# A decoder block's first stage: scale columns queued in a row, x turned by quarters, first weights asked for by GpSimd

## The chip, the cores and the metric

The kernel runs on one core of a Trainium2 chip. The metric is the device time of one execution in microseconds (us); less is better. The core has TensorE (PE, matmuls), VectorE (DVE), ScalarE (ACT), GpSimd (POOL) and SyncE (SP, which here only issues transfers); each works off its own queue in order and waits on semaphores for the others. 16 DMA engines move data between the chip's memory and the core's.

## The reference, cut to what matters

One layer for 512 tokens of width 2048, all in float32: an adaLN modulation, a normalised input, one input projection for two head groups, their mix, an output projection and an MLP. The change lies in the first lines of it.

```python
mod = silu(c) @ w_ada + b_ada            # 6 x 2048: shift, scale, gate for both halves
h = rms_norm(x, norm1_w) * (1 + scale) + shift
z = h @ w_in                             # 2048 -> 7168: q, k, v | q, f, i, g of the second group
...                                      # dilated attention | HGRN2, merged, w_out, gated residual
...                                      # second adaLN, squared-ReLU MLP, gated residual
```

The code names the column of (1 + scale) * norm1_w `g1c` and that of the shift `s1c`, 16 columns of 128 values each.

## The kernel before

**Exact products.** A float32 product is made of three reduced ones: every operand is split into a rounded part (`hi`, `whi`; ScalarE, L336 and L39) and what is left (`lo`, `wlo`; VectorE, L337 and L40), and TensorE adds hi x whi, lo x whi and hi x wlo (`ch_mm`, L206 to L208). Weights come in pairs of 128-row blocks (`load_w`, L189, 512 or 256 columns); the tiles for the rounded and for the remaining part number four each, and a pair of both groups' weights fills them.

**The first stage.** `gemv` makes modulation columns: for a block of columns it loads `w_ada` (L123) and adds 16 row blocks, each times a column of silu(c), on VectorE into two accumulators (the first two rows by L127, the rest by L129). A scale block is 256 columns, 8 loads of 256 KB and 16 VectorE operations; there are eight, and each serves two of the 16 row blocks k of x. `to_cols` turns the accumulators on TensorE (L149), sums them on ScalarE (L152), and `mod_cols` adds the bias and multiplies by the norm's weight on VectorE (L167, L169). x comes in 16 tiles; its squares are summed (L261, L264, L265), the inverse root is a power on GpSimd (L212), the tiles are scaled (L277 on ScalarE, L279 on VectorE), turned (64 transposes, L283) and copied (L285). `scaled(k)` multiplies a turned tile by its column (L335) and splits it.

**The first groups.** `first_groups` runs twice over k = 0..15 in pairs. The first pass takes 512 columns of the forget gate (`prj`) and 256 of the query (`prc`) of the second group, without the shift: 36 matmuls of 128x512 a pair, 288 in all. `before` (`scale_block`) makes the next scale block ahead of each pair. The second pass takes the next columns; during both, the shift columns are made in the background (`bg_step`, `shift_gen`: 512 columns at a time). What the first pass lacked, the shift's part, is made by `shift_through`: a gemv over `w_in`, whose accumulators are added (L143) and turned (L149). Then comes the rest of the input projection with its TensorE order written out by hand, the attention, the recurrence, the output projection and the MLP.

**What sets the order.** A scheduler places the instructions of the first stage in the order of the code, moved by the due times it works out; `tc.issue_after(ins)` holds what is made inside it behind an instruction. Buffers come from pools of fixed sizes, so a load or a split waits for the last reader of the tile that it overwrites. All weight and modulation loads of this stage are issued by SyncE, from one queue.

Of the kernel before, what the change touches and what calls it, by code (L numbers as in the profile page):

```python
# [15 lines left out]
P = 128  # L16
D = 2048
# [27 lines left out]
def hybrid_block(ctx, tc, x, c, positions, norm1_w, w_ada, b_ada, w_in, q_norm_w, k_norm_w,  # L45
# [29 lines left out]
    pool.memset(mhalf, -0.5)  # L75
# [10 lines left out]
    dve.tensor_copy(bcol, ps_c[:, 2 * NK:P])  # L86
    sc = const.tile([P, NK], F32, name="sc")
# [28 lines left out]
    def gemv(view, vec, col0, n=512, early=False):  # L116
# [3 lines left out]
        for k0 in range(0, NK, nk):  # L120
            raw = spare.pop(0) if early and spare else slot("araw") if early else gv.tile([P, 512], F32, name="araw", bufs=4)
            raw = raw.rearrange("p (k n) -> p k n", n=n)
            nc.sync.dma_start(raw, view[:, k0:k0 + nk, col0:col0 + n])  # L123
            for k in range(k0, k0 + nk):
                acc = accs[k % 2]
                if k < 2:
                    dve.tensor_scalar(acc, raw[:, k - k0], vec[:, k:k + 1], None, op0=ALU.mult)  # L127
                else:
                    dve.scalar_tensor_tensor(acc, raw[:, k - k0], vec[:, k:k + 1], acc, op0=ALU.mult, op1=ALU.add)  # L129
# [8 lines left out]
    def to_cols(accs, dst):  # L138

        nb = accs[0].shape[1] // P  # L140
        parts = 1 if nb == 4 else 2
        if parts == 1:
            dve.tensor_tensor(accs[0], accs[0], accs[1], op=ALU.add)  # L143
        yield
        pc = bank("pc")
        for j in range(nb):
            for u in range(parts):
                c = (j * parts + u) * P
                pe.transpose(pc[:, c:c + P], accs[u][:, j * P:(j + 1) * P], ident)  # L149
        for j in range(nb):  # L150
            c = pc[:, j * parts * P:(j + 1) * parts * P]
            act.activation(c, c, AF.Copy, accum_out=dst[:, j:j + 1])  # L152
# [7 lines left out]
    def mod_cols(kind, b, dst, nw, n=512, early=False):  # L160

        for _ in gemv(ada_v, sc, kind * D + b * n, n, early):
            yield
        nb = n // P
# [3 lines left out]
        if nw is not None:  # L168
            mod_cols.last = dve.scalar_tensor_tensor(d, d, 1.0, nw[:, b * nb:(b + 1) * nb], op0=ALU.add, op1=ALU.mult)  # L169
# [16 lines left out]
    def load_w(view, k0, c0, n=512, eng=None, ahead=True, raws=None):  # L186
        with tc.high_priority() if ahead else ExitStack():
            raw = wr.tile([P, 2, n], F32, name="wraw", tag="raw", bufs=4)
            nc.sync.dma_start(raw, view[:, k0:k0 + 2, c0:c0 + n])  # L189
# [20 lines left out]
    def rstd_of(dst, ss, n, inv_n):  # L210
        dve.tensor_scalar(dst, ss, inv_n, EPS, op0=ALU.mult, op1=ALU.add)
        pool.tensor_tensor(dst, dst, mhalf[:, 0:n], op=ALU.pow)  # L212
# [34 lines left out]
    first_scale = mod_cols(1, 0, g1c, n1c, 256, True)  # L247
# [8 lines left out]
    for q in range(4):  # L256
        for ti in range(NT):
            jk = work("jk")
            with tc.issue_after(sc_ready.ins), tc.issue_after(sig_ready.ins):
                if q == 3 and ti % 2:  # L260
                    dve.tensor_tensor_reduce(jk, xs[ti][q], xs[ti][q], op0=ALU.mult, op1=ALU.add, scale=1.0, scalar=0.0,  # L261
                                             accum_out=ssx[:, ti, q:q + 1])
                else:
                    act.activation(jk, xs[ti][q], AF.Square, accum_out=ssx[:, ti, q:q + 1])  # L264
    dve.tensor_reduce(rx, ssx, axis=AX.X, op=ALU.add)  # L265
# [1154 lines left out]
```

## Time and profile before

| | us |
|---|---|
| median of 3 runs | 2300.57 |
| lowest, highest | 2293.37, 2303.32 |
| the profiled execution | 2297.95 |
| its span | 2296.2 |
| TensorE busy | 2224.9 (97%) |
| VectorE busy | 1809.9 (79%) |
| ScalarE busy | 1098.2 (48%) |
| GpSimd busy | 447.3 (19%) |

An engine's queue is in order: an instruction that waits holds up all behind it. The table of groups gives for each kind of instruction its count, its mean duration and the idle time ahead of it with what ended that. In the timeline a row gives start, length, engine, line, operation, what it writes and reads, a count, and in brackets the idle time before it with its releaser. In the windows PEclk is the share of full clock that was granted to TensorE. Consecutive matmuls overlap, so their spacing is taken from starts.

### The profile page before, as it was taken

What the parts mean: (1) busy time and instruction counts of PE and PEld (TensorE: products, weight loads), DVE (VectorE), ACT (ScalarE), POOL (GpSimd) and SP (SyncE); (2) the same over time, 40 slices, a digit from 0 to 9 for tenths busy, and PEclk for the clock granted to TensorE, in tenths of its full rate; (3) what the DMA queues carried; (4) which work ended last, traced back from release to release, by engine and by line L of the source; (5) the groups of instructions that cost most, each with busy time, mean ns of one, the idle gap of its engine ahead of it and who ended that gap; (6) DMA issues with size and microseconds to landing.
All of it is one profiled execution on the core that took longest, in us unless ns stands there. A gap on an engine that the chain in (4) does not pass through costs nothing.

```text
span 2296.2 us, 33105 instructions
## 1 busy us (share of the span) xinstructions
PE 2224.9 (97%) x11769; PEld 1824.4 (79%) x11769; DVE 1809.9 (79%) x2765; ACT 1098.2 (48%) x1950; POOL 447.3 (19%) x664
## 2 busy tenths in 40 slices
PE   4899999999999999999999999999999999999999
PEld 3787877888778888778887888888888888888887
DVE  6999777677876565668648988988897679967878
ACT  5555434433344454447544556555564333343332
POOL 1000022000230000002232323323332222222221
PEclk9999999999999999999999999999999999999999
DMA  9798455556545256746969799889889987998784
GB/s 327 254 335 315 124 177 156 177 160 207 187 151 184 68 173 225 247 152 217 367 231 383 251 344 347 298 306 386 298 328 390 339 293 260 385 344 291 278 301 164
DMA packets 262582, 598.31 MB, mean 261 GB/s; under 512 B 23220, under 2 KB 43968, under 8 KB 262416
## 3 DMA queue, kind: packets, MB, share of 16 engines
q1 hardware_dynamic: 186800, 332.54, 43.1%
q0 software_dynamic: 70720, 254.21, 30.0%
q10 hardware_dynamic: 4896, 9.44, 1.2%
q8 instruction: 93, 1.52, 0.3%
q14 instruction: 73, 0.60, 0.1%
HBM read 518.49 MB, written 77.61 MB: 260 GB/s over the span
## 4 chain that ended last, share of the span: by engine, by line
PE 60%; DVE 17%; DMA 14%; issue 6%; ACT 2%; POOL 1%; SPq 0%; DVEq 0%; ACTq 0%; POOLq 0%
PE f L1177 9%; PE f L1178 9%; PE f L1176 9%; DMA araw<-in_w_ada_dram 6%; PE prj L198 5%; PE prj L199 5%; PE prj L200 5%; DVE vlo L1161 3%; DVE acc L129 3%; DVE raw L1144 2%; PE f L208 2%; PE f L206 2%; PE f L207 2%; DMA Fl<-f_lod 2%; DVE wlo L40 2%
## 5 line engine op out<-in xcount | busy, mean ns | idle before, releaser
L1160 ACT CAST vhi<-raw 128x1024 fp32r<-128x1024 f32 x392 | 413.4, 1055 | 534.5 <-PE f L1178 416.3
L1161 DVE TENSOR_TENSOR vlo<-raw,vhi 128x1024 fp32r<-128x1024 f32 x392 | 475.5, 1219 | 153.5 <-ACT vhi L1160 152.7
L1177 PE MATMUL f<-vlo,Fh 128*128 128x512 f32 x1376 | 537.1, 390 | 3.9 <-DVE vlo L1161 3.8
L1178 PE MATMUL f<-vhi,Fl 128*128 128x512 f32 x1376 | 535.8, 389 | 0.8 <-DMA Fl<-f_lod 0.8
L1176 PE MATMUL f<-vhi,Fh 128*128 128x512 f32 x1376 | 536.1, 390 | 0.0
L39 ACT CAST whi<-wraw 128x512 fp32r<-128x512 f32 (+1 forms) x368 | 219.8, 601 | 453.2 <-PE prj L200 313.3
L198 PE MATMUL prj<-whi,hi 128*128 128x512 f32 x896 | 364.9, 407 | 1.3 <-ACT gg L701 1.3
L200 PE MATMUL prj<-whi,lo 128*128 128x512 f32 x896 | 351.4, 392 | 0.0
L199 PE MATMUL prj<-wlo,hi 128*128 128x512 f32 x896 | 351.0, 392 | 0.0
L40 DVE TENSOR_TENSOR wlo<-wraw,whi 128x512 fp32r<-128x512 f32 (+1 forms) x368 | 243.2, 665 | 120.9 <-ACT whi L39 118.3
L129 DVE SCALAR_TENSOR_TENSOR acc<-araw,sc,acc 128x512 f32<-128x512 f32 (+1 forms) x392 | 252.7, 672 | 100.5 <-DMA araw<-in_w_ada_dram 99.2
L1177 PEld LDWEIGHTS f<-vlo,Fh 128*128 128x128 f32 x1376 | 258.3, 188 | 63.3 <-DVE vlo L1161 10.0
L1178 PEld LDWEIGHTS f<-vhi,Fl 128*128 128x128 f32 x1376 | 258.3, 188 | 54.8 <-DMA Fl<-f_lod 1.6
L1176 PEld LDWEIGHTS f<-vhi,Fh 128*128 128x128 f32 x1376 | 258.3, 188 | 53.5
L1144 DVE TENSOR_TENSOR raw<-raw,raw 128x1024 f32<-128x1024 f32 x224 | 267.7, 1216 | 4.1 <-DMA raw<-in_w_ff_dram 3.9
L198 PEld LDWEIGHTS prj<-whi,hi 128*128 128x128 f32 x896 | 169.3, 189 | 36.5 <-ACT gg L701 1.6
L200 PEld LDWEIGHTS prj<-whi,lo 128*128 128x128 f32 x896 | 168.9, 188 | 36.7
L199 PEld LDWEIGHTS prj<-wlo,hi 128*128 128x128 f32 x896 | 169.5, 189 | 33.0 <-DVE wlo L40 1.0
L1122 POOL DMA_DIRECT2D Fh<-f_hid x112 | 79.0, 705 | 425.9 <-PE f L1178 410.8
L208 PE MATMUL f<-hi,wlo 128*128 128x512 f32 x256 | 99.8, 390 | 1.3 <-DVE wlo L40 1.3
L206 PE MATMUL f<-hi,whi 128*128 128x512 f32 x256 | 100.2, 391 | 0.0
L207 PE MATMUL f<-lo,whi 128*128 128x512 f32 x256 | 99.6, 389 | 0.0
(311 smaller groups left out, 2917.0 us busy)
## 6 DMA issues: line engine op xcount, KB each, us to landing
raw<-in_w_ff_dram SPq DMA_DIRECT2D x224, 512.0 KB, 9.7
araw<-in_w_ada_dram SPq DMA_DIRECT2D x384, 256.0 KB, 4.3
Fh<-f_hid POOLq DMA_DIRECT2D x112, 512.0 KB, 6.5
Fl<-f_lod POOLq DMA_DIRECT2D x112, 512.0 KB, 7.7
wraw<-in_w_in_dram SPq DMA_DIRECT2D x104, 512.0 KB, 4.1
Fh<-h_hid POOLq DMA_DIRECT2D x60, 512.0 KB, 6.6
Fl<-h_lod POOLq DMA_DIRECT2D x60, 512.0 KB, 7.5
f_hid<-part POOLq DMA_DIRECT2D x48, 512.0 KB, 7.9
```

Of the source, the lines that this page charges most:

```text
L39: nc.scalar.copy(hi, src)
L40: (eng or nc.vector).tensor_tensor(lo, src, hi.bitcast(F32), op=ALU.subtract)
L129: dve.scalar_tensor_tensor(acc, raw[:, k - k0], vec[:, k:k + 1], acc, op0=ALU.mult, op1=ALU.add)
L198: pe.matmul(banks[ti], lhsT=hi[:, ts], rhs=whi, start=first, stop=False)
L199: pe.matmul(banks[ti], lhsT=hi[:, ts], rhs=wlo, start=False, stop=False)
L200: pe.matmul(banks[ti], lhsT=lo[:, ts], rhs=whi, start=False, stop=last)
L1144: dve.tensor_tensor(dst, a, b, op=ALU.subtract)
L1160: act.copy(hi, src)
L1161: split_done.append(dve.tensor_tensor(lo, src, hi.bitcast(F32), op=ALU.subtract))
L1176: pe.matmul(banks[t], lhsT=fh[u][a][:, ts], rhs=whi[:, a], start=first, stop=False)
L1177: pe.matmul(banks[t], lhsT=fh[u][a][:, ts], rhs=wlo[:, a], start=False, stop=False)
L1178: pe.matmul(banks[t], lhsT=fl[u][a][:, ts], rhs=whi[:, a], start=False, stop=end)
```

## The change

The eight scale blocks (`scale_cols`) are tied one behind the other: the loads and multiply-adds of a block are held behind the last load and the last multiply-add of the block before. A block's two accumulators are no longer turned; four matmuls with a column of ones sum them straight to columns, and ScalarE writes `g1c` from there with the norm's weight as scale and (1 + bias) times the weight as bias. x is scaled and turned by quarters: k = 0, 1 first, the others behind the scale blocks of the first three pairs; its squares alternate between ScalarE and VectorE, as do the scalings. `hi` is made from the turned tile directly. The weights of both passes of `first_groups` are asked for by GpSimd, but for the first pair, which SyncE asks for behind x. The shift's first steps and the last `shift_through` are held behind earlier work.

```diff
+    def scale_cols(b):
+        steps = gemv(ada_v, sc, D + b * 256, 256, True)
+        for _ in range(NK // 2):
+            with ExitStack() as order:
+                for ins in scale_cols.behind:
+                    order.enter_context(tc.issue_after(ins))
+                next(steps)
+            yield
+        next(steps, None)
+        scale_cols.behind = [gemv.last.ins, gemv.load.ins]
...
+        for j in range(2):
+            for u in range(2):
+                pe.matmul(pc[:, j:j + 1], lhsT=accs[u][:, j * P:(j + 1) * P], rhs=ones, start=u == 0, stop=u == 1)
+        for j in range(2):
+            ks = slice(2 * b + j, 2 * b + j + 1)
+            scale_cols.last = act.activation(g1c[:, ks], pc[:, j:j + 1], AF.Identity, scale=n1c[:, ks],
+                                             bias=b1c[:, ks])
...
-                if q == 3 and ti % 2:
+                if ti % 2:
...
+    def x_turned(k, *anchors):
+        q, j = k // 4, k % 4
+        if j == 0:
+            for ti in range(NT):
+                if ti % 2:
+                    with tc.issue_after(anchors[0].ins):
+                        x_turned.dve = dve.tensor_scalar(xs[ti][q], xs[ti][q], rx[:, ti:ti + 1], None, op0=ALU.mult)
+                else:
+                    with tc.issue_after(anchors[1].ins):
+                        x_turned.act = act.activation(xs[ti][q], xs[ti][q], AF.Copy, scale=rx[:, ti:ti + 1])
...
+    for k in range(2):
+        x_turned(k, sum_ready, last_square)
...
+    with tc.issue_after(x_turned.act.ins), tc.issue_after(x_turned.dve.ins):
+        first_weights = [pair_of_weights(0, 4096, 3072, nc.sync)]
...
+        act.activation(hhi[k], xnT[k], AF.Copy, scale=g1c[:, k:k + 1])
+        a = act.activation(xnT[k], xnT[k], AF.Copy, scale=g1c[:, k:k + 1])
+        scaled.last = dve.tensor_tensor(hlo[k], xnT[k], hhi[k].bitcast(F32), op=ALU.subtract), a
...
-            wt = load_w(win_v, k0, c_f, ahead=False)
-            wc = load_w(win_v, k0, c_q, 256, None, ahead=False)
+            with tc.issue_after(rx_ready.ins):
+                wt, wc = first_weights.pop() if first_weights else pair_of_weights(k0, c_f, c_q, pool)
...
-            run_all(mod_cols(1, k0 // 2 + 1, g1c, n1c, 256, True))
-        for k in (k0, k0 + 1):
-            scaled(k)
+            run_all(scale_cols(k0 // 2 + 1))
+        if k0:
+            for k in (k0, k0 + 1):
+                scaled(k)
+        for k in (range(2, 8), range(8, 12), range(12, 16), (), (), (), (), ())[k0 // 2]:
+            x_turned(k, *scaled.last)
...
-            for _ in range(12):
-                bg_step()
+            with tc.issue_after(scale_cols.last_dve.ins):
+                for _ in range(12):
+                    bg_step()
...
-    later.insert(0, shift_through(4096 + 512))
+    later.insert(0, behind(shift_through(4096 + 512), gemv.load.ins))
```

VectorE's queue from the remaining parts of the third pair's weights (k = 4, 5) to those of the fourth. `wlo` is a weight's remaining part (L40), `lo_687` and `lo_692` before and `lo_649` and `lo_654` after are x's of k = 4 and 5; L127 and L129 before, L131 and L133 after are a scale block's operations. Before:

```order
L337 TENSOR_TENSOR lo_692<-xnT,hi_691 128x512
L40 TENSOR_TENSOR wlo<-wraw,whi 128x512
L129 SCALAR_TENSOR_TENSOR acc<-araw,sc,acc 128x256
L40 TENSOR_TENSOR wlo<-wraw,whi 128x256
L129 SCALAR_TENSOR_TENSOR acc<-araw,sc,acc 128x256
L127 TENSOR_SCALAR acc<-araw,sc 128x256 x2
L40 TENSOR_TENSOR wlo<-wraw,whi 128x256
L129 SCALAR_TENSOR_TENSOR acc<-araw,sc,acc 128x256 x4
L40 TENSOR_TENSOR wlo<-wraw,whi 128x512
L167 TENSOR_TENSOR g1c<-g1c,bcol 128x2
L129 SCALAR_TENSOR_TENSOR acc<-araw,sc,acc 128x256 x4
```

After:

```order
L40 TENSOR_TENSOR wlo<-wraw,whi 128x512 x2
L40 TENSOR_TENSOR wlo<-wraw,whi 128x256
L339 TENSOR_TENSOR lo_649<-xnT,hi_648 128x512
L40 TENSOR_TENSOR wlo<-wraw,whi 128x256
L339 TENSOR_TENSOR lo_654<-xnT,hi_653 128x512
L313 TENSOR_SCALAR xs<-xs,rx 128x512 x2
L40 TENSOR_TENSOR wlo<-wraw,whi 128x512 x2
L40 TENSOR_TENSOR wlo<-wraw,whi 128x256 x2
L131 TENSOR_SCALAR acc<-araw,sc 128x256 x2
L133 SCALAR_TENSOR_TENSOR acc<-araw,sc,acc 128x256 x14
L339 TENSOR_TENSOR lo_788<-xnT,hi_787 128x512
```

Before, the scale blocks' operations stand among the weights' subtractions; after, those of the fourth pair stand together ahead of the whole of block 3, which serves the same pair.

TensorE's queue at the end of the third pair. `pc` holds a scale block's turned accumulators or sums, `prj` and `prc` are the two groups' accumulators, `ptx` is x being turned. Before:

```order
L206 MATMUL prc<-hi_691,whi 128x512
L207 MATMUL prc<-lo_692,whi 128x512
L208 MATMUL prc<-hi_691,wlo 128x512
L149 MATMUL pc<-ident,acc 128x128 x4
L206 MATMUL prj<-hi_795,whi 128x512 x4
L206 MATMUL prc<-hi_795,whi 128x512 x2
```

After:

```order
L242 MATMUL prc<-lo_654,whi 128x512
L243 MATMUL prc<-hi_653,wlo 128x512
L188 MATMUL pc<-mhalf,acc 128x1
L319 MATMUL ptx<-ident,xs 128x128 x4
L188 MATMUL pc<-mhalf,acc 128x1 x3
L319 MATMUL ptx<-ident,xs 128x128 x8
L241 MATMUL prj<-hi_787,whi 128x512 x4
```

Block 3's sums stand at the same place as its transposes did, between the third and the fourth pair; transposes of x stand between them now.

SyncE's queue from the first scale block on (`xs` is x, `araw` a piece of the modulation weights, `wraw` a pair of the projection's). Before:

```order
L123 DMA araw<-in_w_ada_dram 128x2x256 x8
L255 DMA xs<-in_x_dram 128x512 x16
L123 DMA araw<-in_w_ada_dram 128x2x256 x8
L189 DMA wraw<-in_w_in_dram 128x2x512
L189 DMA wraw<-in_w_in_dram 128x2x256
L123 DMA araw<-in_w_ada_dram 128x2x256 x8
```

After:

```order
L127 DMA araw<-in_w_ada_dram 128x2x256 x8
L291 DMA xs<-in_x_dram 128x512 x16
L224 DMA wraw<-in_w_in_dram 128x2x512
L224 DMA wraw<-in_w_in_dram 128x2x256
L127 DMA araw<-in_w_ada_dram 128x2x256 x56
L127 DMA araw<-in_w_ada_dram 128x512 x64
```

After the first pair no weight stands among the scale and shift loads; the other 30 weight loads of both passes stand in GpSimd's queue behind the power operation.

## Rows read from the trace of the kernel before

**Rows 1.** The page: span, and busy time and share of each engine.

```profile
span 2296.2 us, 33105 instructions
PE 2224.9 (97%) x11769; PEld 1824.4 (79%) x11769; DVE 1809.9 (79%) x2765; ACT 1098.2 (48%) x1950; POOL 447.3 (19%) x664
```

**Rows 2.** Windows: length, busy PE, PEld, DVE, ACT, POOL; clock, DMA share, GB/s.

```profile
30.00:52.00 22.00, 18.99 (x107) 16.18 (x105) 21.70 (x56) 16.67 (x38) 0.00 (x0) 1.00 1.09 361
...
104.00:140.00 36.00, 36.00 (x164) 29.52 (x163) 27.29 (x78) 21.41 (x48) 4.75 (x8) 1.00 0.69 228
140.00:210.00 70.00, 69.30 (x309) 56.26 (x307) 69.36 (x121) 41.25 (x92) 0.53 (x1) 1.00 1.01 363
```

**Rows 3.** Waits of PE, 0 to 260 us: total, times, longest.

```profile
PE ptx L283 <- ACT xs L277: 12.8, 1, 12.8
...
PE prj L206 <- ACT hi L336: 6.9, 3, 4.1
```

**Rows 4.** Timeline of PE, 36 to 215 us.

```profile
36.80 1.21 PE L206 MATMUL prj<-hi,whi 128*128 128x512 f32 x4 [0.90 <-ACT hi L336]
...
43.13 1.91 PE L283 MATMUL ptx<-ident,xs 128*128 128x128 f32 x16
...
69.47 0.27 PE L149 MATMUL pc<-ident,acc 128*128 128x128 f32 x1
70.37 0.55 PE L149 MATMUL pc<-ident,acc 128*128 128x128 f32 x3 [0.63 <-DVE acc L129]
70.67 1.17 PE L206 MATMUL prj<-hi,whi 128*128 128x512 f32 x4
...
80.08 1.07 PE L206 MATMUL prj<-hi,whi 128*128 128x512 f32 x4
80.99 0.62 PE L206 MATMUL prc<-hi,whi 128*128 128x512 f32 x2
...
94.20 2.08 PE L206 MATMUL prj<-hi,whi 128*128 128x512 f32 x4 [4.06 <-ACT hi L336]
...
98.84 0.53 PE L207 MATMUL prj<-lo,whi 128*128 128x512 f32 x1
...
113.58 0.27 PE L768 MATMUL ps_v<-ident,rows 128*128 128x128 f32 x1
113.78 0.22 PE L769 MATMUL ps_v<-ident,posf 4*128 4x4 f32 x1
...
214.17 1.11 PE L149 MATMUL pc<-ident,acc 128*128 128x128 f32 x4 [4.86 <-DVE acc L143]
```

**Rows 5.** Windows around the two waits, columns as in rows 2.

```profile
96.00:98.00 2.00, 2.00 (x6) 1.18 (x5) 2.00 (x4) 1.65 (x4) 0.00 (x0) 0.50 0.03 10
...
216.00:218.00 2.00, 2.00 (x6) 1.59 (x5) 1.76 (x4) 1.97 (x3) 0.00 (x0) 0.50 1.06 387
```

**Rows 6.** Timeline of SyncE's queue, at 90 us.

```profile
90.20 29.70 SPq L189 DMA_DIRECT2D wraw<-in_w_in_dram  x7
```

**Rows 7.** Timeline of DVE; groups of ACT and DVE by form, to 108 us.

```profile
84.82 0.87 DVE L129 SCALAR_TENSOR_TENSOR acc<-araw,sc,acc 128x256 f32<-128x256 f32 x2
85.62 0.68 DVE L40 TENSOR_TENSOR wlo<-wraw,whi 128x512 fp32r<-128x512 f32 x1
86.22 0.87 DVE L129 SCALAR_TENSOR_TENSOR acc<-araw,sc,acc 128x256 f32<-128x256 f32 x2
...
L335 ACT ACTIVATE xnT<-xnT,g1c 128x512 f32<-128x512 f32 x15 | 10.2, 719 | 5.5 <-DVE g1c L169 5.5
...
L127 DVE TENSOR_SCALAR acc<-araw,sc 128x256 f32<-128x256 f32 x13 | 4.1, 347 | 0.0
```

**Rows 8.** Timeline of DVE: last scale block's end, and the shift sums' addition.

```profile
107.22 0.16 DVE L169 SCALAR_TENSOR_TENSOR g1c<-g1c,n1c 128x2 f32<-128x2 f32 x1
...
213.43 0.68 DVE L143 TENSOR_TENSOR acc<-acc 128x512 f32<-128x512 f32 x1
```

**Rows 9.** The page's DMA issues: KB each, us to landing.

```profile
Fl<-f_lod POOLq DMA_DIRECT2D x112, 512.0 KB, 7.7
```

## What was predicted

> **What bounds the kernel now.** The profiled execution took 2297.95 us (span 2296.2, [rows 1]); the median of the three runs is 2300.57, 2.62 us more, and every difference worked out below is put on that median. I read the busy shares first: TensorE has work for 97% of the span [rows 1], so only what keeps it idle or slow can move the end. Then I read the order. From the 732nd of the changed kernel's 10,683 TensorE instructions on (in the projection behind the second pass) the order is the same before and after, and the other engines' queues hold the same work in almost the same places; what the first 220 us gain or lose is therefore handed on to the end.
>
> Inside those 220 us the windows show VectorE all but full from 30 us on (21.70 of 22.00 in 30–52) while TensorE works beside it; VectorE has slack only in 104–140 (27.29 of 36) and is full again in 140–210 [rows 2]. The list of TensorE's waits names what it waits for: the scaled x (12.8 us, ahead of its first work) and hi after a scale block (6.9 in three waits, the longest 4.1) [rows 3]; and once more, at 214.17, the addition that closes the shift sums of the first forget group, 4.86 us [rows 4]. After both longer waits (4.06 us before 94.20, 4.86 before 214.17) the granted clock was 0.50, the 1.2 GHz level [rows 5]. At that level the ten products from 94.20 take until 98.84, 4.64 us, where at the spacing of 80.08 to 80.99 (four in 0.91) they take 2.28 [rows 4]: such a wait costs its length and about 2.3 us more. SyncE's queue stands for 29.70 us from 90.20 behind weight loads without a free buffer [rows 6], with the DMA share at 0.03 in 96–98 [rows 5].
>
> The DMA engines are no bound of the new order. By the shapes, x (4.2 MB), the scale columns (16.8) and the first pass's weights (6.3) are 27.3 MB, and at the 361 GB/s of [rows 2] that is 76 us; the pass ends at 113.58 [rows 4].
>
> **The change part by part.** The durations: a 128x256 multiply-add of a scale block starts 0.40 us after the one before it (two in the 0.80 from 84.82 to 85.62) and a 128x512 subtraction takes 0.60 (85.62 to 86.22) [rows 7]. A block is 2 multiplies (at most 0.35 each) and 14 multiply-adds: 0.7 + 5.6 = 6.3 us.
>
> *Sums by products with ones.* Removed are 16 small VectorE operations of at most 0.16 us [rows 8], 2.6 us at most, and 32 transposes. New are 32 products with one column, which no row shows: between 0.05 and the 0.22 of a 4x4 transpose [rows 4], against 0.12 for a transpose (16 in 1.91 at 43.13 [rows 4]). I take 0.1: no difference on TensorE. More is saved in the round trip: before, TensorE stood 4.06 us from block 5's transposes to the product with its hi (94.20 [rows 4]), VectorE finishing the column behind queued multiply-adds. Now ScalarE writes the column itself; two short activations and one 0.72 us scaling [rows 7] make it 1.7 to 2.1 us.
>
> *x by quarters, squares on two engines.* VectorE loses 6 scalings and 14 tiny operations and gets 6 squares, about 5 us less work up to block 7. The first product no longer waits for the copies of most of x: two scalings on ScalarE, four transposes, two copies, the first weights and hi after the power operation give 33.0 us against 36.80. From there to the end of the third pair (k = 4, 5): 108 products at 0.2275 (24.6), 40 transposes at 0.12 (4.8), 1.0 for the sums, 2.65 waiting for block 1 and 1.1 in short waits like the 0.63 at 70.37 give 67.2, against 69.47 [rows 4]. A **lead of 2.3 us**.
>
> *Scale blocks one behind the other.* Here the order decides. Before, block 3's multiply-adds stood among the splits of earlier weights, and VectorE worked on them while TensorE multiplied. Now all 16 operations of block 3 stand behind the four weight splits of k = 6, 7. A split subtracts what ScalarE rounded, and there are four rounded tiles, one pair's worth: ScalarE can't write the next pair's before TensorE has read the last of k = 4, 5. So VectorE stands during the third pair and begins block 3 at about 67.6, TensorE has nothing until about 73.5 (6.3 us idle), and hi is there at 75.5, against 70.67 before [rows 4]: the lead of 2.3 becomes a **lag of 4.8**. What hid block 3 was the third pair's products; that cover is gone. A wait of 6.3 is longer than the two that dropped the clock, so up to 2.3 more: the fourth pair ends at 75.5 + 9.2 = 84.7 to 87.0, against 80.08. Block 4 has five multiply-adds behind a split that waits for the end of that pair: 4.3 us idle, 1.8 to hi. Blocks 5 to 7 wait 2.2, 0.8 and 1.45. The first pass ends 35 us after the fourth pair, at 119.7 to 122, against 113.58 [rows 4]: **6 to 8 us behind**.
>
> *Back to VectorE.* The last scale block is done about 29 us after the fourth pair, at 115 (before 107.22) [rows 8]. From there to the addition that closes the forget group's shift sums the order holds the same work less about 2 us. Before this took from 107.22 to 214.03, 106.8 us, 4 of them idle; after it takes 104 to 106, so it ends at 219 to 221, or 5 to 7 later than 214.03. TensorE comes there at about 216 and waits 3 to 5, as now (4.86), so the slow clock that follows can be saved: **3.5 to 6 us later** than before, 4.5 in the middle.
>
> *Weights asked for by GpSimd.* Each load waits for a split two pairs earlier and is one pair (8 to 9 us) ahead of its use. GpSimd's loads land after 7.7 us late in the kernel [rows 9]; that is covered in the first pass, where pairs last over 9. The second pass needs 36 x 0.2275 = 8.2 us a pair: there the cost lies between 0 and 8 pairs x 1 us. I take 0 (a load that also has its split's 2 us ahead of it stays near 8), and keep 8 for the range. What the row of SyncE's 29.70 us shows is order, not the time of issuing: loads that could run stand behind one that can't.
>
> The Trainium skill ("Trainium Kernel Development and Optimization", Key Constraints) says that DMAs from SP, ACT and POOL share 16 DMA engines and that issuing from several saves only the sequencer's issue time. By that rule this part would gain nothing beyond issue time; the trace agrees on the shared engines only in so far as they are full in 30–52 (share 1.09 [rows 2]), and its 29.70 us of blocked queue speak for a gain that the rule leaves out, which is the first rival below.
>
> *Shift loads and `behind`.* The shift loads follow the scale loads on SyncE with no weight load between; their 16.8 MB come early enough in either order. Cost zero, hidden by VectorE's own queue.
>
> **Rivals.** *Queue freed, VectorE never starved (faster).* If VectorE finds work during the third pair after all, its 5 us less work, the 9 us idle of 104–140 [rows 2] and the freed loads come forward. The addition would be done at 200, and TensorE, with the first product 3.8 us earlier and its waits of 0.63, 4.06 and a slow clock's 2.3 gone, would arrive at 198 to 203: 11 to 17 us faster, 2284 to 2290. For it speaks [rows 6]; against it, that the order on an engine is fixed and block 3 stands behind the split.
>
> *Every scale block pays, and the loads too (slower).* Place: blocks 3 to 6 and the second pass. If the clock drops after block 3 and also after block 4's 4.3 us (4.06 did it before), and the second pass runs at the time of a GpSimd load, then 2 x 2.3 + up to 8 come on top of 4.5: 12 to 17 us slower, 2312 to 2318. It decides from a load-to-product time over 8.2 us in the second pass.
>
> *Nothing passes through (same).* The splits wait so often in both orders that the start at 33.0 and the stalls cancel: within 3 us, 2298 to 2304.
>
> **How the numbers follow.** Forecast, 3.5 to 6 later: 2304 to 2307, middle 2305, chance 0.45. Nothing passes through: 0.13. Faster rival 0.22, slower rival 0.20. The range takes in the forecast and reaches to the near part of both rivals, 2288 to 2315. A measurement of this kernel can tell about 0.5%, 11.5 us, from no change, that is 2289 and 2312. Nearly all of the faster rival lies below 2289 (0.20 with its edge left out), nearly all of the slower one above 2312 (0.19), the rest between (0.61).
>
> **What would show it.** Right: a TensorE wait of about 6 us for the first scale sum after the third pair, near 67, with VectorE's multiply-adds of block 3 running through it and a granted clock of 0.50 behind it; a second wait of about 4 near 85; the first pass ending near 120; the wait for the shift addition served near 220. The first product near 33, SyncE without a stand of tens of us, the sums' products at 0.1 us. Wrong: VectorE busy on block 3 before 60 us (faster rival), or weight splits in the second pass waiting for loads from GpSimd (slower rival). If the addition comes later but the end doesn't move, the step "handed on to the end" was wrong.

## The result, and the profile after

The changed kernel takes 2308.65 us (median of 9 runs, 2304.74 to 2314.91), the kernel before 2301.74 in the same comparison (9 runs, 2293.37 to 2303.88). The ratio is 1.0036 with a 95% interval of 1.0020 to 1.0052: 6.9 us slower by the medians (8.3 by the ratio), within the 0.5% that the prediction called no change. The profiled execution took 2308.65 us, 10.7 more than the profiled one of before.

The page of the changed kernel, to be read against [rows 1]. The columns are as there.

```profile
span 2306.9 us, 33174 instructions
PE 2230.4 (97%) x11801; PEld 1832.2 (79%) x11801; DVE 1811.2 (79%) x2756; ACT 1096.8 (48%) x1928; POOL 467.1 (20%) x695
```

The shares hardly differ from [rows 1]. Of the 10.7 us that the span grew, TensorE is busy for 5.5, working at a slow clock and on longer sums as shown below, and idle for 5.2. The windows (length, then busy time of PE, PEld, DVE, ACT and POOL, then granted clock, DMA share and GB/s) show where the first of it was lost. Two windows of before, beside those of [rows 2]:

```profile
52.00:70.00 18.00, 17.27 (x77) 13.92 (x77) 18.00 (x48) 9.39 (x22) 0.00 (x0) 1.00 1.09 354
70.00:90.00 20.00, 18.45 (x83) 14.44 (x83) 20.00 (x51) 9.58 (x24) 0.00 (x0) 1.00 1.05 350
```

The changed kernel:

```profile
52.00:70.00 18.00, 16.37 (x85) 13.42 (x83) 8.44 (x20) 10.08 (x20) 3.68 (x5) 1.00 0.39 112
70.00:90.00 20.00, 13.88 (x60) 11.71 (x60) 12.80 (x31) 7.25 (x14) 0.79 (x2) 0.74 0.72 224
90.00:104.00 14.00, 11.24 (x47) 9.56 (x47) 14.00 (x36) 4.29 (x8) 1.45 (x2) 0.76 1.07 343
...
140.00:210.00 70.00, 70.00 (x318) 57.95 (x317) 68.06 (x121) 44.01 (x103) 11.52 (x19) 1.00 0.93 331
```

VectorE, full in 52–90 before, is busy for 8.44 of 18 us in 52–70 and 12.80 of 20 in 70–90; TensorE then has 13.88 of 20 at a mean granted clock of 0.74. In 140–210 both are all but full, as before. TensorE's timeline has the two places (start, length, instruction, count; in brackets the idle time before it and what ended it), then the ones that answer to 113.58 and 214.17 in [rows 4].

```profile
33.80 2.08 PE L241 MATMUL prj<-hi,whi 128*128 128x512 f32 x4 [1.87 <-ACT hi L337]
...
74.86 0.56 PE L188 MATMUL pc<-mhalf,acc 128*128 128x1 f32 x2 [6.48 <-DVE acc L133]
75.27 1.09 PE L319 MATMUL ptx<-ident,xs 128*128 128x128 f32 x4
...
78.90 2.06 PE L241 MATMUL prj<-hi,whi 128*128 128x512 f32 x4
...
91.47 1.83 PE L188 MATMUL pc<-mhalf,acc 128*128 128x1 f32 x8 [2.73 <-DVE acc L133]
94.60 2.08 PE L241 MATMUL prj<-hi,whi 128*128 128x512 f32 x4 [1.29 <-ACT hi L337]
...
124.21 0.27 PE L827 MATMUL ps_v<-ident,rows 128*128 128x128 f32 x1
...
221.60 0.66 PE L151 MATMUL pc<-ident,acc 128*128 128x128 f32 x4 [2.28 <-DVE acc L145]
```

Block 3's sums wait 6.48 us, block 4's 2.73 and its hi another 1.29; four products take 2.06 and 2.08 us behind these waits, where at full clock [rows 4] has 1.07. VectorE's timeline around the first wait shows what it did instead of block 3.

```profile
64.28 0.69 DVE L40 TENSOR_TENSOR wlo<-wraw,whi 128x512 fp32r<-128x512 f32 x1 [0.22 <-ACT whi L39]
67.94 0.42 DVE L40 TENSOR_TENSOR wlo<-wraw,whi 128x256 fp32r<-128x256 f32 x1 [2.96 <-ACT whi L39]
68.61 0.43 DVE L40 TENSOR_TENSOR wlo<-wraw,whi 128x256 fp32r<-128x256 f32 x1 [0.25 <-ACT whi L39]
68.95 0.61 DVE L131 TENSOR_SCALAR acc<-araw,sc 128x256 f32<-128x256 f32 x2
69.48 5.62 DVE L133 SCALAR_TENSOR_TENSOR acc<-araw,sc,acc 128x256 f32<-128x256 f32 x14
```

It stood 2.96 us for the rounded part of a weight of the fourth pair, which ScalarE could not write before TensorE was through with the third, and only then ran block 3 in one piece, 68.95 to 75.10.

**One account for all that follows.** VectorE's time up to the end of the addition that closes the shift's sums is 30 us, plus its busy time from there, plus its idle time. A window over just this stretch gives the three; first before, then the changed kernel (its DVE column is the third busy time).

```profile
30.00:214.03 184.03, 169.95 (x769) 137.95 (x767) 174.39 (x385) 105.25 (x233) 5.29 (x9) 0.98 0.92 317
```

```profile
30.00:221.46 191.46, 176.42 (x798) 145.13 (x798) 168.78 (x364) 107.49 (x225) 25.58 (x38) 0.96 0.85 289
```

VectorE has 5.6 us less to do up to there (168.78 against 174.39) and stands idle for 22.7 us instead of 9.6. The 13.0 more of idle time less the 5.6 of work are the 7.4 by which the addition is late.

The 5.6 us are for the most part not saved but put off. In the new order 22 instead of 29 multiply-adds of the gemv over `w_in` stand ahead of the addition, first before, then the changed kernel (count, then busy time, mean ns, idle time before):

```profile
L129 DVE SCALAR_TENSOR_TENSOR acc<-araw,s1c,acc 128x512 f32<-128x512 f32 x29 | 20.3, 736 | 0.0
```

```profile
L133 DVE SCALAR_TENSOR_TENSOR acc<-araw,s1c,acc 128x512 f32<-128x512 f32 x22 | 15.8, 746 | 1.4 <-DMA araw<-in_w_in_dram 1.4
```

That is 4.5 of the 5.6. What the change itself takes from VectorE comes out near nothing: six scalings and 16 small operations gave back 5.2 us, six squares cost 4.2 and their sums 0.5. In the whole kernel VectorE is busy for 1.3 us more (1811.2 against the 1809.9 of [rows 1]).

### The profile page after: what moved, and what is told of

Its sections match the earlier page's. It is cut to its first block, busy times and chain, and to the rows that moved or that the text cites. A ratio compares the mean times of both kernels' runs of the same rounds, so it can differ in the third digit from the quotient of the medians.

```text
span 2306.9 us, 33174 instructions
## 1 busy us (share of the span) xinstructions
PE 2230.4 (97%) x11801; PEld 1832.2 (79%) x11801; DVE 1811.2 (79%) x2756; ACT 1096.8 (48%) x1928; POOL 467.1 (20%) x695
## 4 chain that ended last, share of the span: by engine, by line
PE 55%; issue 15%; DMA 15%; DVE 9%; POOL 4%; ACT 1%; SPq 0%; POOLq 0%; DVEq 0%; ACTq 0%
PE f L1237 8%; PE f L1236 8%; PE f L1235 8%; DMA araw<-in_w_ada_dram 7%; PE prj L233 5%; PE prj L235 5%; PE prj L234 5%; DMA f_lod<-fs 3%; DVE acc L133 3%; PE f L243 2%; PE f L242 2%; PE f L241 2%; DMA f_hid<-part 2%; DVE wlo L40 2%; PE prj L241 1%
## 5 line engine op out<-in xcount | busy, mean ns | idle before, releaser
L40 DVE TENSOR_TENSOR wlo<-wraw,whi 128x512 fp32r<-128x512 f32 (+1 forms) x368 | 243.1, 666 | 120.7 <-ACT whi L39 114.7
L133 DVE SCALAR_TENSOR_TENSOR acc<-araw,sc,acc 128x512 f32<-128x512 f32 (+1 forms) x392 | 251.2, 673 | 104.2 <-DMA araw<-in_w_ada_dram 103.3
```

The costliest lines, as they stand in the source:

```text
L40: (eng or nc.vector).tensor_tensor(lo, src, hi.bitcast(F32), op=ALU.subtract)
L133: gemv.last = dve.scalar_tensor_tensor(acc, raw[:, k - k0], vec[:, k:k + 1], acc, op0=ALU.mult, op1=ALU.add)
```

## Experiments

All were timed against the kernel before on the same chip; ratios are to it, with a 95% interval. The changed kernel's is 1.0036. The table gathers what the readings below use: where VectorE's addition ended, its idle time from 30 us to there, and VectorE's waits for background columns of the modulation in 250 to 690 us (its multiply-adds' waits for `araw` from `w_ada`). These columns and all rows come from one profiled execution each; those of e6 and e8 took 2310.35 and 2313.35 us, 8.0 and 7.7 above their medians.

| kernel | addition ends | idle before it | waits, 250–690 | ratio (interval) |
|---|---|---|---|---|
| before | 214.1 | 9.6 | 55.0 | 1 |
| changed | 221.6 | 22.7 | 64.4 | 1.0036 (1.0020–1.0052) |
| e1, splits behind their block | 212.7 | 14.5 | 60.1 | 1.0013 (1.0002–1.0024) |
| e2, x turned at once | 214.6 | 16.5 | 58.9 | 1.0013 (1.0000–1.0026) |
| e3, weights by SyncE | 224.3 | 25.0 | 60.6 | 1.0060 (1.0046–1.0075) |
| e4, blocks not tied | 221.4 | 22.3 | 59.1 | 1.0058 (1.0043–1.0073) |
| e5, e1 and e2 | 214.2 | 16.2 | 59.6 | 1.0025 (1.0015–1.0036) |
| e6, e1, x in two goes | 217.0 | 17.8 | 59.7 | 1.0017 (1.0005–1.0028) |
| e7, e1, last gemv free | 225.5 | 20.3 | 57.8 | 1.0038 (1.0025–1.0050) |
| e8, ones alone | 218.1 | 14.6 | 62.0 | 1.0031 (1.0017–1.0044) |
| e10, e1, scaling by ScalarE | 212.2 | 15.8 | 54.8 | 0.9999 (0.9991–1.0008) |
| e11, e1, rests by GpSimd | 221.4 | 17.8 | 57.5 | 1.0051 (1.0037–1.0065) |
| e12, weights by GpSimd alone | 215.5 | 10.1 | 55.5 | 0.9996 (0.9987–1.0005) |

### The order on VectorE (e1)

```diff
-            with tc.issue_after(rx_ready.ins):
+            with tc.issue_after(rx_ready.ins), tc.issue_after(scale_lasts[k0 // 2] if k0 > 4 else rx_ready.ins):
                 wt, wc = first_weights.pop() if first_weights else pair_of_weights(k0, c_f, c_q, pool)
```

`scale_lasts` holds each block's last multiply-add, so the edge is on VectorE alone; no buffer, load or amount of work differs. In the traces VectorE's order parts from the changed kernel's at these splits, and that of the other engines only later: TensorE's at the sums of block 5 (behind 102.90 us in the changed kernel, 89.34 in e1), ScalarE's at 104.1 (90.0 in e1).

> The changed kernel, and nothing else moved than this: on VectorE the weight splits of pairs k = 6, 7 and later stand behind the last operation of the scale block that serves the same pair. Theory A (the fixed order on VectorE: block 3 stands behind splits that wait for TensorE to finish the third pair, in four rounded tiles): block 3 is summed before the third pair ends, the wait of 6.48 us at 74.86 falls below 2 us, the first pass ends at 114 to 118 instead of 124.2, the addition at 221.6 comes 4 to 7 us earlier, the time falls by 5 to 9 us to about 2300 to 2304. Theory B (SyncE stands 19.7 us for tiles that hold x until it is turned, so block 4's loads come late whatever VectorE's order is): the stall only moves to block 4, where TensorE then waits 4 us or more, and the time falls by less than 3 us.

Measured: 2299.93 us, ratio 1.0013. TensorE's waits in 0 to 260 us (total, times, longest):

```profile
PE pc L191 <- DVE acc L133: 14.2, 3, 11.3
...
PE prj L244 <- ACT hi L340: 4.1, 3, 1.9
...
PE pc L151 <- DVE acc L145: 2.7, 1, 2.7
```

Of the 14.2 for sums, 11.3 are the first block's, ahead of all work; what is left for the others is 2.9, where the changed kernel had 6.48 at block 3 alone. Block 3's sums follow the third pair at once:

```profile
67.17 0.28 PE L191 MATMUL pc<-mhalf,acc 128*128 128x1 f32 x2
```

The granted clock is 1.00 from 30 to 90. Theory A is shown for blocks 3 and 4: up to there nothing but the place of these subtractions differs, the stall is gone, and the last product before the orders part comes 13.6 us earlier (89.34 against 102.90; 1.0 us of it is an earlier start, 28.91 against 29.96 for the first transposes). SyncE still stood 19.7 us for tiles that hold x, and no new stall of 4 us came at block 4, so theory B is not the cause. Behind that the scheduler also placed later sums anew, with waits of 0.95 and 1.51 us at 92.94 and 96.10 and a clock of 0.53 in 98–100. The addition ends 8.9 us earlier, at 212.7 (4 to 7 were expected), and by the ratios two thirds of the loss are back (0.23 of 0.36%; the intervals just overlap).

### How x is turned (e2, e5, e6)

```diff
-        for k in (range(2, 8), range(8, 12), range(12, 16), (), (), (), (), ())[k0 // 2]:
+        for k in (range(2, 16), (), (), (), (), (), (), ())[k0 // 2]:
```

e5 has this edit and e1's. e6 has e1's and `range(2, 12), range(12, 16)` here.

> The changed kernel with x scaled and turned in one go behind the first pair (k = 2 to 15 together) instead of by quarters behind the blocks of three pairs; VectorE's order moves with it, block 3 then stands among the splits. Theory B (tiles held by x stop SyncE's queue): the stand of 19.7 us goes, loads of blocks 3 to 7 come in a row, TensorE's waits at blocks 3 and 4 vanish, the first pass ends at 112 to 116, the time is 6 to 10 us below the changed kernel's. Theory A alone: the same, since the order moves as well, but no better than the run with the splits behind their block. If neither order nor tiles matter: within 3 us of the changed kernel.

> Both edits of the first two runs at once: the splits of each pair behind the scale block that serves it, and x turned in one go. Theory A+E (the order on VectorE was the stall; what the mended order still loses is VectorE's idle time of 5.9 us in 52 to 70, because block 4's loads stand 19.7 us for tiles that hold x): VectorE's idle time in 52 to 90 falls below 3 us, the addition for the shift comes at 207 to 211 (212.71 with the order alone), the time is 2293 to 2298, 2 to 5 us below the run with the order alone. Theory F (the order alone already takes all that can be had here, because later VectorE waits for background loads at a pace of their own): the addition is earlier but the time stays within 2 us of 2299.9.

> The splits behind their block, and x turned in two goes (k = 2 to 11 behind the first pair's block, 12 to 15 behind the next) instead of three. Theory A+E: SyncE's stand of 19.7 us is about halved, block 4's loads come some 10 us earlier, the first pass ends at 104 to 107, the addition for the shift at 208 to 212, the time 1 to 4 us below the order alone. Theory F: within 2 us of 2299.9.

Measured: e2 1.0013, e5 1.0025, e6 1.0017. In e2 the scheduler itself put block 3 among the splits, and the stall went as in e1, by another way: turning x by quarters had moved the order, and the order made the stall. The loads did come earlier (SyncE's longest stand for x is 8.9 us in e2, 10.0 in e5 and 15.9 in e6, where half of 19.7 was expected). But theory E fell: VectorE's idle time before the addition is 16.5 and 16.2 us, more than e1's 14.5, and e5 and e6 are no better than e1. A window of e5 shows why.

```profile
52.00:70.00 18.00, 18.00 (x98) 15.02 (x97) 9.53 (x23) 10.96 (x22) 1.44 (x2) 1.00 0.81 263
```

TensorE is full in 52–70, with the last 28 of the 56 transposes of x among its work (the other 28 stand at 44.77 and 48.40), and VectorE idle for 8.5 of 18 us: its splits wait for TensorE, which turns x first (4.09 us of it before the split at 60.36). Block 1's sums also wait longer (3.54 us at 44.55, 1.40 at 41.87 in e1), since six more scalings stand ahead of them on VectorE. The loads were not what it lacked.

### Who asks for the weights (e3, e12)

e3 gives the changed kernel's weight loads back to SyncE:

```diff
-                wt, wc = first_weights.pop() if first_weights else pair_of_weights(k0, c_f, c_q, pool)
+                wt, wc = first_weights.pop() if first_weights else pair_of_weights(k0, c_f, c_q, nc.sync)
```

e12 gives those of the kernel before to GpSimd:

```diff
-            wt = load_w(win_v, k0, c_f, ahead=False)
-            wc = load_w(win_v, k0, c_q, 256, None, ahead=False)
+            queue = pool if k0 or c_f > 4096 else nc.sync
+            with tc.issue_after(rx_ready.ins):
+                wt = load_w(win_v, k0, c_f, ahead=False, queue=queue)
+                wc = load_w(win_v, k0, c_q, 256, None, ahead=False, queue=queue)
```

> The changed kernel with the first groups' weights asked for by SyncE again, all else as it is. Theories A and B: weights then stand behind scale loads that wait for x's tiles, so the time is the same or up to 10 us more, and block 3's wait of about 6.5 us stays. Theory C (loads by GpSimd land late and cost the second pass): 4 to 8 us faster, with fewer waits for weight splits in 125 to 200 us.

> The kernel before with one part of the change alone: the first groups' weights asked for by GpSimd, but for the first pair. Theory K (the faster rival's premise: SyncE's stand of 29.70 us at 90.20 leaves VectorE without work in 104 to 140): the stand goes, VectorE's 8.7 us idle in 104 to 140 fall below 4, the addition for the shift comes 3 to 8 us before 214.17, the time is 3 to 8 us below before's. Theory F (on VectorE the fixed order decides, and what is gained ahead of the addition is not kept): the stand goes, the addition moves by less than 3 us, the time stays within 3 us of before's.

Measured: e3 1.0060, block 3's wait 9.45 us; e12 0.9996. GpSimd's loads cost nothing in the second pass (TensorE is busy for 70.00 of 70 us in 140–210 of the changed kernel), and within the changed kernel they seem to help (1.0036 with them, 1.0060 without; the intervals overlap a little): in e3 block 3's multiply-adds wait 2.6 us for their loads and ScalarE once 5.7 us for a weight's. Alone they are worth nothing, and e12 says why. SyncE's row there, beside [rows 6]:

```profile
79.99 50.22 SPq L123 DMA_DIRECT2D araw<-in_w_ada_dram  x24
```

The queue no longer stands for a weight; it stands for the next tile of modulation weights (20.5 us at the longest), since 24 loads run ahead of the multiply-adds that free their tiles. The account of VectorE is that of before:

```profile
30.00:215.39 185.39, 167.53 (x765) 134.68 (x763) 175.31 (x385) 104.93 (x232) 25.80 (x37) 0.99 0.93 315
```

175.31 busy, 10.1 idle, the addition 1.4 us later than before. The premise of the faster rival, that SyncE's stand of 29.70 us costs time, does not hold: the stand is gone and VectorE's idle time is not (10.1 us, 9.6 before), so the loads were not what it stood for. The Trainium skill ("Trainium Kernel Development and Optimization", Key Constraints) has issuing from several engines save issue time alone; e12, at 0.9996, agrees.

### The ties between blocks, and the sums by themselves (e4, e8)

e4 leaves out the loop over `scale_cols.behind` in the changed kernel. e8 puts `scale_cols`, without it, in the place of `mod_cols` for the scale blocks of the kernel before:

```diff
-    first_scale = mod_cols(1, 0, g1c, n1c, 256, True)
+    first_scale = scale_cols(0)
...
-            run_all(mod_cols(1, k0 // 2 + 1, g1c, n1c, 256, True))
+            run_all(scale_cols(k0 // 2 + 1))
```

> The changed kernel without the ties between scale blocks (each block's loads and multiply-adds may go where the scheduler puts them); block 3 still stands behind the splits of the fourth pair, 3 multiply-adds earlier than the last of them. Theory A: block 3's wait stays at 5 to 7 us and the time within 4 us of the changed kernel's. Theory D (the ties themselves cost the time): block 3's wait goes and the time is 5 us or more lower.

> The kernel before with one part of the change alone: the scale blocks' accumulators summed by products with a column of ones and the column written by ScalarE. As in the working of the prediction: the way from the sums to hi falls from 4.06 us of waiting to about 2, the waits at 94.20 and the slow clock behind it (2.3 us) shrink, VectorE loses at most 2.6 us of small work; the time is 2 to 6 us below before's. Rival: VectorE stays the bound of the shift addition at 214, so the time is within 2 us of before's.

Measured: e4 1.0058 with block 3's wait at 4.02 us and block 4's at 3.31, below the 5 to 7 that were expected at block 3, but with the slow clock behind both (0.76 in 70–90, 0.74 in 90–104): not the ties cost the time. e8 1.0031, where my working had 2 to 6 us of gain and its rival no change. The way from the sums to hi is about as short as expected (a wait of 2.41 us), but the scheduler placed the shorter column anew, and two waits for hi stood elsewhere:

```profile
70.86 2.08 PE L223 MATMUL prj<-hi,whi 128*128 128x512 f32 x4 [2.41 <-ACT hi L353]
...
115.93 2.07 PE L223 MATMUL prj<-hi,whi 128*128 128x512 f32 x4 [3.94 <-ACT hi L353]
```

Each left the slow clock behind (0.50 in 70–74 and in 116–118; 2.08 and 2.07 us for four products), VectorE's idle time before the addition rose from 9.6 to 14.6 us, and the addition came 4.0 later.

### VectorE's work (e10, e11)

e10 is e1 with x's last three quarters scaled by ScalarE; e11 is e1 with the second 256-column weight of a pair split by GpSimd.

```diff
-                if ti % 2:
+                if ti % 2 and q == 0:
                     with tc.issue_after(anchors[0].ins):
                         x_turned.dve = dve.tensor_scalar(xs[ti][q], xs[ti][q], rx[:, ti:ti + 1], None, op0=ALU.mult)
```

```diff
-                load_w(win_v, k0, c_q, 256, None, ahead=False, queue=queue))
+                load_w(win_v, k0, c_q, 256, pool if k0 else None, ahead=False, queue=queue))
```

> The splits behind their block, and x's last three quarters scaled by ScalarE alone: six operations of about 0.41 us, 2.4 us in all, fewer on VectorE in 36 to 62. Theory H (behind the mended order the work of VectorE up to the addition for the shift is the bound): the addition comes 1.5 to 2.5 us before 212.71 and the time is 1 to 3 us below 2299.9. Theory B (what counts on VectorE is its waiting for block 4's loads, not its work): the addition stays within 1 us of 212.7.

> The splits behind their block, and of each pair's two 256-column weights the second one's remaining part made by GpSimd: 15 subtractions of 0.34 us, 5.1 us in all, fewer on VectorE in both passes, 2.4 of them before the first pass ends; on GpSimd one takes 1 to 2 us, by the 0.53 us of its 128x64 products. Theory H: the addition comes 3 to 5 us before 212.71, the time is 3 to 5 us below 2299.9, near 2295. Rival J (GpSimd's queue, where the subtraction stands between weight loads, delays these, and TensorE waits for them in the second pass): the addition is no earlier and the time 0 to 6 us higher.

Measured: e10 2297.08 us, 0.9999, the best of the changed ones and level with before (2297.24). Its account is mixed:

```profile
30.00:212.09 182.09, 171.56 (x794) 139.88 (x793) 166.31 (x358) 110.12 (x229) 24.85 (x37) 0.99 0.88 303
```

1.8 us less work than e1 and 1.3 us more idle time: the addition moved by 0.5, as theory B had it, while the time by the ratios fell by 0.14% (3 us), as H had it. The intervals of e1 and e10 overlap (1.0002 to 1.0024, 0.9991 to 1.0008), and what the two profiles differ by lies mostly far behind the addition: at the same product e10 is 1.1 us ahead of e1 at 690 us and 6.6 at 2000. So a gain from the lighter VectorE is not shown.

e11 is at 1.0051. GpSimd's 14 subtractions took 1342 ns each, and VectorE, with those taken from it, was busy for longer (173.56 us up to the addition, 168.12 in e1). In part that is order again: 26 instead of 22 multiply-adds of the gemv over `w_in` stand ahead of the addition, 3.1 us. In part its own operations got longer. The same groups, first e1, then e11 (columns: instructions, then busy time, mean ns, idle time before):

```profile
L133 DVE SCALAR_TENSOR_TENSOR acc<-araw,sc,acc 128x512 f32<-128x512 f32 x56 | 40.1, 743 | 0.0
```

```profile
L133 DVE SCALAR_TENSOR_TENSOR acc<-araw,sc,acc 128x512 f32<-128x512 f32 x56 | 42.7, 794 | 0.0
```

Rival J's result came (the addition no earlier, and a loss against e1 of 0.38%, more than the 0 to 6 us it had), though not by late loads alone.

### The last gemv, and before once more (e7, e9)

```diff
-    later.insert(0, behind(shift_through(4096 + 512), gemv.load.ins))
+    later.insert(0, shift_through(4096 + 512))
```

> The splits behind their block, and the last of the three gemvs over the input weights no longer held behind the earlier loads; its loads go where the scheduler puts them (the first four ahead of the scale blocks' last 40). Theory G (the 4 to 5 us that every run with the change loses between 300 and 690 us come from that gemv's late loads, which push the background columns later on VectorE): the lead over before at 250 us is kept at 690 us to within 1.5 us, the time is 2294 to 2298. Theory F or E: the loss between 300 and 690 us stays at 4 us or more; four early loads of 256 KB take tiles from the scale blocks and cost 0 to 5 us, the time is 2299 to 2305.

> The kernel before, unchanged, for a second profile. Theory I (the 4 to 5 us that TensorE loses between 300 and 690 us in every run against the first profile of before are that profile's luck, one of the fast executions): this profile lags behind the first by 3 us or more at 690 us although its first 250 us are the same within 1 us. Theory F (they belong to the change, which leaves VectorE with more background work): it stays within 1.5 us of the first profile up to 690 us.

e7 (with e1's edit): 1.0038. Its gemv went ahead of the other background work, VectorE had 175.17 us to do before the addition, and this ended at 225.5; theory G finds no support, for TensorE's lag grew again, from 10.6 us at 300 to 12.9 at 690. e9, a second profile of before (2294.65 us, one execution), is 1.0 us ahead of the first at 206 us and 1.5 at 690: theory I finds no support either. Between 300 and 690 us e12 loses nothing against the first profile of before; the changed kernel loses 6.8 us, e8 6.6, and the others 1.2 (e3) to 6.4 (e6).

## Why the prediction came out right, step by step

**The lead** was 1.1 us instead of 2.3: the first product was at 33.80 (33.0 forecast), the third pair ended at 68.38 (67.2), 74.86 less the wait of 6.48, against 69.47. That the sum came out so near is in part luck, for two of its terms were wrong by about the same, one each way. The wait for block 1 was 0.39 us, not 2.65. And the first products were slow: four took 2.08 us where [rows 4] has 1.21, and those behind them start 0.43 us apart until 39.33, so that 12 products took 5.53 us where 0.2275 each makes 2.7. That is near the spacing at a clock of 0.50 (ten products in the 4.64 us from 94.20, [rows 4] and [rows 5]), but the granted clock in 34 to 40 is 1.00, so the reason is not shown. Before, transposes stood in this place, and they were slow too (28 in 5.59 us at 29.49, where 16 at 43.13 took 1.91).

**The sums' products** took 0.20 us each, not the 0.1 that no row had shown, and one of the signs of being right failed with that. Between other work the four of a block (the trace has two records for each) hold TensorE for 0.81 us:

```profile
103.13 0.94 PE L188 MATMUL pc<-mhalf,acc 128*128 128x1 f32 x8
103.94 0.49 PE L242 MATMUL prj<-lo,whi 128*128 128x512 f32 x1
```

By this 32 of them take 6.5 us, where the 32 transposes that they replace take 3.8 at 0.12: an estimate of 2.6 us more on TensorE, where I had no difference.

**Block 3** is the step on which the forecast rested, and it held: 6.48 us of waiting (6.3 forecast), for the reason given, as e1 shows. The slow clock came behind it, as the sum allowed. Mis-sized is what follows the wait: the first product with hi stood at 78.90, not 75.5. The four sums and 12 transposes of x that lie between ran at the 1.2 GHz level (0.50 in 74 to 78), 4.0 us where I had put 2.0. So the lag was 8.2 us instead of 4.8.

**Block 4** waited 2.73 and 1.29 us (4.3 and 1.8 forecast), but its wait, too, dropped the clock (0.50 in 94 to 98), which I had left to the slower rival; its four sums took 1.83 us. Blocks 5 to 7, for which I had 2.2, 0.8 and 1.45 us, waited for nothing. The position of 113.58 came at 124.21, 10.6 us late, where I had 6 to 8. It is not the end of the first pass, as I had it, but that of the seventh of eight pairs (168 of 192 `prj` products lie ahead of it, before and after); the two positions are alike all the same, and the pass ends 10.7 us late.

**Back to VectorE** came out best, the addition's end at 221.5 (219 to 221), but again not by its terms. From the last scale block to that end I had 106.8 us before, 4 of them idle, and 2 us less work after. Before, 7.5 us of that stretch were idle (VectorE is busy for 99.19 of 106.73 us). After, it has 2.0 us more work (101.15 of the 104.16 us from 117.30) and 3.0 us idle. What shrank is idle time, not work. Then it went as forecast: TensorE waited 2.28 us (3 to 5), without a slow clock behind it, which before's 4.86 had. That gives back what TensorE had lost: at the same product it was 10.0 us behind before at 206 us, ahead of the wait, and 5.4 at 240, inside the forecast of 3.5 to 6.

**Handed on to the end** is the step that failed in size. The lag of 5.4 us grew to 12.8 at 690, fell to 8.8 at 1005 and was 10.8 at the end in these two profiles; by the medians it is 6.9. The growth stands in TensorE's waits for the recurrence's operands in 250 to 690 us. First before (total, times, longest), then the changed kernel:

```profile
PE pC L648 <- DVE z L601: 3.8, 3, 2.8
PE pB L574 <- DVE z L601: 3.5, 2, 2.4
```

```profile
PE pB L633 <- DVE z L660: 6.5, 4, 3.7
PE pC L707 <- DVE z L660: 6.1, 5, 1.9
```

VectorE, which makes them, stands longer in that stretch for the background columns' loads, 64.4 us instead of 55.0:

```profile
DVE acc L133 <- DMA araw<-in_w_ada_dram: 64.4, 49, 4.2
```

I had argued that the same order from there on hands on the same lag. It does not. VectorE works off a queue in which background columns stand ahead of TensorE's operands, so a late load could delay these. That this is the cause is not shown. For it speaks that before and its second profile, and e10 and e12, whose medians show no loss, wait 54.8 to 55.5 us there, and all that lost wait 57.5 to 64.4. Against it speaks that VectorE's idle time in 250 to 690 as a whole did not grow (100.9 us before, 98.4 after; its waits for ScalarE's rounded weights fell from 25.1 to 18.4), that a load lands 3.4 us after its issue in both (median), and that the waits do not give the loss (e3 waits 60.6 and loses 1.2 us in 300 to 690, e10 waits 54.8 and loses 2.7). Why the lag grows is open: neither the last gemv's tie (e7) nor the first profile's luck (e9) explains it, and no run moved these loads alone.

**GpSimd's loads** cost 0, as taken (e12, and TensorE's full 140 to 210 us). **The faster rival** had the premise wrong (e12). **The slower rival** had one part right, the clock behind block 4, and the second pass wrong. **Nothing passes through** (within 3 us) is ruled out by the interval, whose lower end of 0.20% is 4.6 us. The time is inside the range (2288 to 2315); against the 4.5 us in the middle of the forecast the medians show 6.9. The mechanism at block 3 is right and shown; that the sum lies as near as it does owes something to errors that cancel, in the lead and on the way back to VectorE.

## What to carry to other kernels

Where several engines work off fixed queues, what a rewrite does is decided by the place at which each instruction comes to stand: e1 took back about two thirds of the loss by one edge on one engine, and e8 turned a shorter way from the sums to hi into a loss. Before trusting a part that saves work, add up the busy and the idle time of the engine that gates the next stage, and ask whether less work ahead of a point is work saved or work put off; here VectorE had 5.6 us less ahead of the addition, 4.5 of them put off, and stood 13.0 longer. A stall that lets TensorE's clock fall also slows whatever stands just behind it, so the wait itself understates its price.

## What the runs showed of the hardware

GpSimd's arithmetic slows VectorE's beside it. In e11 the 128x512 multiply-adds took 794 ns on average instead of 743, and the whole difference is in a few: up to the addition, seven took 1.22 to 1.32 us, each while one of GpSimd's subtractions ran, and those beside which GpSimd did no arithmetic took 0.74. One of them, two multiply-adds taking 1.89 us together, and the subtraction beside it:

```profile
147.65 2.13 POOL L40 TENSOR_TENSOR wlo<-wraw,whi 128x256 fp32r<-128x256 f32 x1 [1.57 <-ACT whi L39]
```

```profile
149.11 1.89 DVE L133 SCALAR_TENSOR_TENSOR acc<-araw,sc,acc 128x512 f32<-128x512 f32 x2
```

The trace of before shows it too: while GpSimd makes its products at 125.19 to 129.94 a subtraction takes 0.81 us, right after 0.68.

```profile
127.25 2.69 POOL L822 TENSOR_TENSOR rot_w<-cosT,rw 128x64 f32<-128x64 f32 x4
```

```profile
128.96 0.81 DVE L40 TENSOR_TENSOR wlo<-wraw,whi 128x512 fp32r<-128x512 f32 x1
129.69 0.81 DVE L143 TENSOR_TENSOR acc<-acc 128x512 f32<-128x512 f32 x1
130.41 0.47 DVE L127 TENSOR_SCALAR acc<-araw,sc 128x512 f32<-128x512 f32 x1
130.81 0.68 DVE L40 TENSOR_TENSOR wlo<-wraw,whi 128x512 fp32r<-128x512 f32 x1
```

TensorE's clock fell to 0.50 behind waits of 6.48 us and of 2.73 with 1.29 close behind it, and not behind one of 2.28 (1.00 in 212 to 222), all in one execution. In e8 it fell behind one of 2.41 (0.50 in 70 to 74). So the length of a wait alone does not tell, by these rows, whether the clock falls. And a product with a single column is not free: three sums (six records) at 76.16 took 1.28 us at the slow level, three at 56.17 took 0.72 at full clock.
